# Two-layer streaming encoder on one core: product-key gates in spans of 3, 5, 8 and of 8, 8 blocks, and the scoring pools at the other end of SBUF

## The chip, the core and the metric

The kernel runs on one core of one Trainium2 chip. Its engines are TensorE (PE; its weight loads are listed apart as PEld), VectorE (DVE), ScalarE (ACT), GpSimd (POOL), which here only issues indirect transfers, and SyncE (SP), which issues the others. The metric is the device time of one execution in microseconds (us). [...]

## The reference, cut to what matters

Each of two layers is a mixer (attention, mLSTM, chunk MLP) and then a product-key expert layer (`peer`) over 16384 experts. Each token scores 2 x 128 sub-keys in 8 heads, takes the best 16 experts of each head, and adds a gated sum of their rows:

```
s = jnp.einsum('thcd,hckd->thck', q, keys)
v1, i1 = lax.top_k(s[:, :, 0], PEER_TOPK)
v2, i2 = lax.top_k(s[:, :, 1], PEER_TOPK)
...
e = i1[ci // 16] * 128 + i2[ci % 16];  g = softmax(vs)
act = gelu(einsum('thkd,td->thk', u_tab[e], xi))
y   = einsum('thk,thkd->td', g * act, v_tab[e])
```

There are 512 prompt tokens (four blocks of 128, b0 to b3) and 64 sample tokens (s). Everything is float32.

## The kernel before

**Two ways through the expert layer.** In each layer one pair of prompt blocks (b0 and b1 in layer 0, b2 and b3 in layer 1) meets all experts *densely*: the 16384 experts are 128 chunks of 128, and for each chunk TensorE makes H (eight products of a 128x128 piece of `U` with the tokens), ScalarE the gelu `A`, VectorE `A * W` with the gate block `W` (L1077), and TensorE adds `A`'s products with the chunk of `V` into `y` (L1084). Each chunk loads 512 KB of `U` and 512 KB of `V`. The other tokens *gather*: 64 pairs (s) or 128 pairs (a block) of rows from `peer_u` and from `peer_v`, 512 KB at a time, through four row buffers (`gath`). POOL issues a gather when a row buffer is free; VectorE multiplies the row (L964 for u, L976 for v) and so frees it. That is 640 gathers a layer.

**The gates.** A gate block `W` holds the gates of 8 chunks for 256 tokens. `gate_batch` builds, for 8 tokens, a one-hot of the second index (`o2`, 128x1024, L1002), one of the first index over the chunks of a *span* of blocks (`o1`, L1003) and its product with the gate (L1005); TensorE multiplies the two (L1009, 16 products), and ScalarE copies the result to each block of the span (L1011). 32 batches make a span, so `o2` and the 16 products are made once for each batch of each span, however many blocks it has. Before the change both layers have five spans (`QB`): of 1, 3, 4, 4, 4 and of 2, 2, 4, 4, 4 blocks. `first_gate` builds the first span ahead of the chunks; each further one is woven into the last `WIN` = 16 chunks of the span before it.

**Order.** A scheduler of the language fixes each engine's order at build time; every engine runs its list in that order. Gathers have low priority and fill the places that the scheduler's own clock leaves them. VectorE's list therefore holds the gathers' multiplies between the gates, the selection and the chunks' multiplies, and each waits for what stands ahead of it. Calls of `behind` add that a chunk's multiply stands after the last gate batch issued ahead of it.

**Layer 0**: mixer; `first_gate`; 8 chunks of the dense loop woven with `scores` of b2 and b3 (16 rounds of products, and `select_heads` on VectorE, L894 to L905); `finish_select`; the other 120 chunks. Gathers of s, b2 and b3 run beside it and on into layer 1's mixer. **Layer 1**: mixer; `scores` of b2 and b3 with 24 leads (H and gelu of the first chunks, 16 of them kept in `pre`); `first_gate`; 128 chunks. Gathers of s, b0 and b1 run beside it. Last comes `final` (a norm and a store) for each token block.

The tiles of `scores` and of the selection stand in the pool `select`, which is open through the whole program, and in `xg2`, `tmp2` and `wts2`.

Of the kernel before, what the change touches and what calls it, by code (L numbers as in the profile page):

```python
# [21 lines left out]
P = 128  # L22
DM = 1024
# [13 lines left out]
WT = 1056  # L37
TD = 256
NG = TD + NS
QB = [[1, 3, 4, 4, 4], [2, 2, 4, 4, 4]]  # L40
WIN = 16
LOW = 10 ** 7
PS_TAG = {"p": "mm", "a": "mm", "r": "mm", "o": "o", "tp": "tr", "ta": "tr", "tr": "tr"}
PS_BUFS = {"mm": 4, "tr": 3, "o": 1}
T_TAG = {"p": "t", "a": "t", "r": "tr"}
T_BUFS = {"t": 4, "tr": 2}
DENSE_T = 4
# [68 lines left out]

# Tokens go in groups: g1 = two prompt blocks and the sample, g2 = two prompt blocks. In each layer one pair of
# prompt blocks meets all experts densely (gates built from one-hot products); the other tokens gather their rows.
class Build:
    def __init__(self, ctx, tc, h, outs):  # L120
        self.tc, self.nc, self.h, self.o = tc, tc.nc, h, outs
        ec = ctx.enter_context
        self.cp = ec(tc.tile_pool(name="const", bufs=1))
        self.lp = ec(tc.tile_pool(name="layer", bufs=1))
        self.ca = ec(tc.tile_pool(name="carry", bufs=1))
        self.gp = ec(tc.tile_pool(name="gath", bufs=4))
        self.sm = ec(tc.tile_pool(name="small", bufs=2))
        self.dp = ec(tc.tile_pool(name="dram", bufs=1, space=DRAM))
        self.sp = ec(tc.tile_pool(name="select", bufs=1))

# [14 lines left out]
    def dense_pools(self, ec, l):  # L145
        tc = self.tc

        def pool(name, bufs, **k):
            return ec(tc.tile_pool(name=name, bufs=bufs, reuse_waits="tile", **k))
        self.dx = pool("xd", 1)  # L150
        self.up = pool("ustream", 2)
        self.vp = pool("vstream", 2)
        self.da = pool("act", 2)
        self.xg = pool("xg2", 1)
        self.t2 = pool("tmp2", DENSE_T)
        self.wp = pool("wts2", 3)
        self.whp = None
        self.wb = pool("gate", 5)
        self.d2 = pool("onehot", 2)
        self.py = pool("py", 1, space=PSUM)  # L160
        self.ph = pool("ph", 1, space=PSUM)
        self.pm = pool("pmm2", 1, space=PSUM)
        self.mixer = False

# [60 lines left out]

# [1 line left out]
    def setup(self):  # L227
# [92 lines left out]

# [278 lines left out]
    def mlstm(self, l, L, g):  # L599
# [65 lines left out]
        for sl, n in spans:  # L665
            w = sl.stop - sl.start
# [3 lines left out]
        for i, t in sorted(enumerate(g), key=lambda z: -1 if z[1].sample else z[0]):  # L670
            n, a, b = t.n, t.c0, t.c0 + t.n
# [21 lines left out]
            for hh in range(NH):  # L693
                c, r0 = hh // 2, (hh % 2) * HD
# [22 lines left out]
        for sl, n in spans:  # L717
            w = sl.stop - sl.start
# [12 lines left out]
        for sl, n in spans:  # L731
            w = sl.stop - sl.start
# [46 lines left out]

# [1 line left out]
    def scores(self, l, L, g):  # L781
# [231 lines left out]

    def gate_block(self, b):
        pool, tag = (self.wb, "W") if b % 6 else (self.ca, "W0")
        W = pool.tile([P, 8, TD], F32, tag=tag, name=tag)
        return W

    def first_gate(self, l):
        nb = QB[l][0]  # L1020
        self.W0 = [self.gate_block(i) for i in range(nb)]
        hots = None
        if nb == 1:
            hot = self.wb.tile([P, 4, P, 8], F16, tag="W", name="hot")
            o1s = hot[:, 3].rearrange("p i t -> p (i t)")
            hots = [(hot[:, i], o1s[:, 192 * i:192 * i + 192].rearrange("p (a i t) -> p a i t", a=3, i=8)) for i in range(3)]
        for t0 in range(0, TD, 8):
            self.gate_batch(self.W0, 0, t0, self.psum([8, 8 * nb]), hots and hots[t0 // 8 % 3])
            self.gated = self.mark
            yield  # L1030

    def peer_dense(self, l, group, xT):
        nc, h, lag = self.nc, self.h, LAG[l]
        ys = [self.py.tile([P, 2, 512], F32, tag=f"y{i}", name=f"y{i}") for i in range(len(group))]
        hh = self.ph.tile([P, 2, TD], F32, tag="H", name="H")
        pbs = self.ph.tile([P, 2, 8, 32], F32, tag="pb", name="pb")
        acts, pre, nl = [], [], 0
# [64 lines left out]
    def run(self):  # L1102
# [146 lines left out]
```

## Time and profile before

| what | value |
|---|---|
| three timed runs, median | 3788.93 us (3788.86 to 3792.08) |
| profiled execution, first to last instruction | 3795.5 us |
| PE / DVE / ACT / POOL busy | 3337.5 / 2703.0 / 713.3 / 1497.2 us |
| moved by the DMA engines | 1060.62 MB, mean 279 GB/s |

The profiled execution's own time is its span, 3795.5 us; it is 6.6 us (0.17%) above the median of the timed runs, and nothing more is listed around it. A busy share is an average over stages with different limits; the table of stages among the rows below is the view to start from. On POOL one instruction (x) is one gather.

### The profile page before, as it was taken

What the parts mean: (1) busy time and instruction counts of PE and PEld (TensorE: products, weight loads), DVE (VectorE), ACT (ScalarE), POOL (GpSimd) and SP (SyncE); (2) the same over time, 40 slices, a digit from 0 to 9 for tenths busy, and PEclk for the clock granted to TensorE, in tenths of its full rate; (3) what the DMA queues carried; (4) which work ended last, traced back from release to release, by engine and by line L of the source; (5) the groups of instructions that cost most, each with busy time, mean ns of one, the idle gap of its engine ahead of it and who ended that gap; (6) DMA issues with size and microseconds to landing.
All of it is one profiled execution on the core that took longest, in us unless ns stands there. A gap on an engine that the chain in (4) does not pass through costs nothing.

```text
span 3795.5 us, 48023 instructions
## 1 busy us (share of the span) xinstructions
PE 3337.5 (88%) x16456; PEld 2328.2 (61%) x16456; DVE 2703.0 (71%) x6490; ACT 713.3 (19%) x2594; POOL 1497.2 (39%) x1284
## 2 busy tenths in 40 slices
PE   8989889899999999979847787587758999999998
PEld 6767568667676676644524554266634766767764
DVE  4555877998667576555786997789887765766754
ACT  5444222111011011002211212121111111101100
POOL 0000004444444444445555245544565444444442
PEclk9999979899999999989868896698867999999999
DMA  5232227888999999999878698888888899999996
GB/s 178 97 107 70 88 79 259 309 308 301 368 329 326 362 318 348 362 330 328 269 254 303 227 340 249 294 292 305 274 282 276 307 352 337 321 352 335 324 368 247
DMA packets 299956, 1060.62 MB, mean 279 GB/s; under 512 B 36372, under 2 KB 39232, under 8 KB 299712
## 3 DMA queue, kind: packets, MB, share of 16 engines
q0 software_dynamic: 184320, 671.17, 50.3%
q1 hardware_dynamic: 115392, 386.38, 28.6%
q8 instruction: 131, 2.15, 0.2%
q14 instruction: 113, 0.93, 0.1%
HBM read 1048.09 MB, written 8.27 MB: 278 GB/s over the span
## 4 chain that ended last, share of the span: by engine, by line
PE 56%; DVE 16%; DMA 16%; issue 7%; POOL 4%; ACT 1%; SPq 0%; POOLq 0%; DVEq 0%; ACTq 0%
PE H L1044 19%; PE y L1084 19%; DMA row<-in_peer_v_dram,idx 8%; DMA row<-in_peer_u_dram,idx 5%; PE ps L381 5%; PE pb L1009 5%; DVE row L964 4%; POOL row L940 4%; PE ps L392 2%; DVE x_b L976 2%; DMA U<-in_uT_dram 1%; DMA V<-in_peer_v_dram 1%; PE ps L1009 1%; DVE x_s L976 1%; DVE i L895 1%
## 5 line engine op out<-in xcount | busy, mean ns | idle before, releaser
L940 POOL DMA_INDIRECT row<-in_peer_u_dram,idx x640 | 740.2, 1157 | 1439.6 <-DVE row L964 730.9
L940 POOL DMA_INDIRECT row<-in_peer_v_dram,idx x640 | 756.8, 1182 | 814.4 <-DVE x_b L976 452.4
L964 DVE SCALAR_TENSOR_TENSOR row<-row,xn 128x1024 f32<-128x1024 f32 x640 | 777.0, 1223 | 209.4 <-DMA row<-in_peer_u_dram,idx 206.4
L1084 PE MATMUL y<-V,A 128*128 128x512 f32 x1920 | 883.7, 603 | 15.9 <-DMA V<-in_peer_v_dram 12.1
L976 DVE SCALAR_TENSOR_TENSOR x_b<-row,hb,x_b 128x1024 f32<-128x1024 f32 x512 | 656.0, 1281 | 206.9 <-DMA row<-in_peer_v_dram,idx 203.1
L1084 PEld LDWEIGHTS y<-V,A 128*128 128x128 f32 x1920 | 361.8, 194 | 381.2 <-issue 357.9
L1044 PE MATMUL H<-xT,U 128*128 128x256 f32 x2048 | 482.6, 388 | 30.7 <-DMA U<-in_uT_dram 17.6
L1044 PE MATMUL H<-xTd,U 128*128 128x256 f32 x2048 | 478.9, 385 | 1.0 <-DMA U<-in_uT_dram 1.0
L1044 PEld LDWEIGHTS H<-xT,U 128*128 128x128 f32 x2048 | 391.3, 194 | 112.8 <-issue 43.4
L1044 PEld LDWEIGHTS H<-xTd,U 128*128 128x128 f32 x2048 | 388.2, 193 | 84.7 <-issue 38.7
L1009 PEld LDWEIGHTS <-o 128*128 128x128 f16 x4608 | 330.7, 161 | 158.7 <-DVE o L1005 76.8
L392 PE MATMUL ps<-xT,w 128*128 128x320 f32 (+1 forms) x1280 | 344.5, 425 | 38.3 <-DMA w<-in_wt_dram 18.8
L1002 DVE TENSOR_TENSOR o<-jj,sel 128x1024 f16<-128x1024 f16 x288 | 198.8, 691 | 201.0 <-PE pb L1009 169.7
L1009 PE MATMUL pb<-o,o 128*128 128x32 f16 (+2 forms) x4096 | 299.1, 235 | 39.9 <-DVE o L1005 31.9
L392 PEld LDWEIGHTS ps<-xT,w 128*128 128x128 f32 x1280 | 249.4, 199 | 109.3 <-ACT ssg L823 17.0
L1053 ACT ACTIVATE A<-H 128x256 f32<-128x256 f32 x240 | 92.1, 384 | 1012.4 <-PE H L1044 803.7
L1011 ACT ACTIVATE W<-pb 128x64 f32<-128x64 f32 x928 | 151.6, 289 | 668.6 <-PE pb L1009 611.1
L1077 DVE TENSOR_TENSOR A<-A,W 128x256 f32<-128x256 f32 x240 | 98.8, 425 | 139.0 <-ACT A L1053 130.7
L976 DVE SCALAR_TENSOR_TENSOR x_s<-row,hb,x_s 128x1024 f32<-128x1024 f32 x128 | 163.8, 1280 | 43.6 <-DMA row<-in_peer_v_dram,idx 43.0
L381 PE MATMUL ps<-w,xT 128*128 128x512 f32 (+3 forms) x320 | 128.5, 553 | 5.3 <-DMA w<-in_wn_dram 5.3
L336 DVE TENSOR_TENSOR wl<-w,wh 128x1024 fp32r<-128x1024 f32 (+1 forms) x56 | 64.4, 1150 | 76.5 <-PE ps L381 56.8
L381 PE MATMUL ps<-w,mix 128*128 128x512 f32 (+1 forms) x224 | 110.3, 646 | 5.6 <-DMA w<-in_wn_dram 4.0
(319 smaller groups left out, 3201.7 us busy)
## 6 DMA issues: line engine op xcount, KB each, us to landing
V<-in_peer_v_dram SPq DMA_DIRECT2D x256, 512.0 KB
U<-in_uT_dram SPq DMA_DIRECT2D x256, 512.0 KB
w<-in_wt_dram SPq DMA_DIRECT2D x96, 512.0 KB
w<-in_wn_dram SPq DMA_DIRECT2D x80, 512.0 KB
row<-in_peer_u_dram,idx POOLq DMA_INDIRECT x640
row<-in_peer_v_dram,idx POOLq DMA_INDIRECT x640
w<-in_keysT_dram SPq DMA_DIRECT2D x16, 256.0 KB
w<-in_wn_dram SPq DMA_DIRECT2D x8, 264.0 KB
```

The source lines that it names most:

```text
L381: self.nc.tensor.matmul(p[:t.n, :wd], x[kk][:, t.c0:t.c0 + t.n], ww[:, k * wd:(k + 1) * wd], start=(kk + part + j == 0), stop=(kk == KC - ...
L392: self.nc.tensor.matmul(ps, ww[:, k * P:(k + 1) * P], x[k][:, :n], start=(k + part + j == 0), stop=(k == KC - 1 and part == pair and j == ...
L940: self.nc.gpsimd.indirect_dma_start(out=row, out_offset=None, in_=self.h[tab], in_offset=bass.IndirectOffsetOnAxis(ap=t.idx[:, k:k + 1], a ...
L964: nc.vector.scalar_tensor_tensor(row, row, 1.0, xn, op0=ALU.mult, op1=ALU.mult, accum_out=hb[:, k:k + 1])
L976: op = nc.vector.scalar_tensor_tensor(x, row, t.hb[:, k:k + 1], x, op0=ALU.mult, op1=ALU.add)
L1002: nc.vector.tensor_tensor(o2, self.jj, self.sel[:, 1, None, t0:t0 + 8].to_broadcast([P, P, 8]), op=ALU.is_equal)
L1009: nc.tensor.matmul(pb[:, j, :nq], o2[:, :, j], o1[:, p, :, j], start=(p == 0), stop=(p == 1))
L1011: nc.scalar.activation(W[:, :, t0:t0 + 8].rearrange("p i t -> p t i"), pb[:, :, 8 * i:8 * i + 8], AF.Copy, scale=1.0 / GSCALE)
L1044: mm = nc.tensor.matmul(hp, U[:, k, :], xT[k], start=(k == 0), stop=(k == KC - 1))
L1053: nc.scalar.activation(a, hp, AF.Gelu)
L1077: gated = nc.vector.tensor_tensor(a, a, Ws[ci // 8][:, ci % 8, :], op=ALU.mult)
L1084: nc.tensor.matmul(ys[i][:, hf, :], a[:, i * P:(i + 1) * P], V[:, hf * 512:(hf + 1) * 512], start=(c == 0), stop=(c == NCH - 1))
```

## The change

Layer 0 now has three spans (3, 5, 8 blocks) and layer 1 two (8, 8); windows are 16 and 24 chunks in layer 0 and 24 in layer 1. `HOME` names a pool for each block: `0` the carried one, `a` the pool `gate` (5 buffers), `b` a new pool `gate2`. `gate2` is opened by `close_scores`, right after `finish_select`, where `select`, `xg2`, `tmp2` and `wts2` stood, and these now lie at the right end of SBUF. The one-hot `o1` of all batches but layer 0's first span is a tile of `gate2` too. A batch's PSUM tile now comes from the general tag, of three banks instead of two; the bank `pb` is gone. `first_gate` of layer 0 has four one-hot buffers instead of three.

```diff
-QB = [[1, 3, 4, 4, 4], [2, 2, 4, 4, 4]]
-WIN = 16
+QB = [[3, 5, 8], [8, 8]]
+WIN = [[16, 24], [24]]
+GATE_A, GATE_B = 5, [6, 5]
+HOME = ["0aaaaabbbbbb0aaa", "0aaabbbbbaa0aaab"]
...
+    def select_pool(self):
+        self.sel_es = ExitStack()
+        self.sp = self.sel_es.enter_context(self.tc.tile_pool(name="select", bufs=1, side="right", reuse_waits="tile"))
...
-        self.wb = pool("gate", 5)
+        self.wb = pool("gate", GATE_A)
...
+        ec = self.sel_es.enter_context
+        self.xg = pool("xg2", 1, side="right")
+        self.t2 = pool("tmp2", DENSE_T, side="right")
+        self.wp = pool("wts2", 3, side="right")
+
+    def close_scores(self, ec, l):
+        self.sel_es.close()
+        self.wb2 = ec(self.tc.tile_pool(name="gate2", bufs=GATE_B[l], side="right", reuse_waits="tile"))
...
-        ps = self.pm.tile([P] + list(shape), F32, tag=tag, name="ps", bufs=PS_BUFS[tag] if self.mixer else 2)
+        ps = self.pm.tile([P] + list(shape), F32, tag=tag, name="ps", bufs=PS_BUFS[tag] if self.mixer else 3)
...
-            o1 = self.d2.tile([P, 3, 32, 8], F16, tag="o1", name="o1")[:, :, :nq, :]
+            o1 = self.wb2.tile([P, 3, 64, 8], F16, tag="o1", name="o1", bufs=2)[:, :, :nq, :]
...
-        pbs = self.ph.tile([P, 2, 8, 32], F32, tag="pb", name="pb")
...
-            win = min(WIN, nq)
+            win = WIN[l][q] if more else 0
...
-                    self.gate_batch(nxt, c - ci + nq, 8 * done, pbs[:, done % 2])
+                        nxt = [self.gate_block(l, c // 8 - ci // 8 + nb + i) for i in range(QB[l][q + 1])]
+                    self.gate_batch(nxt, c - ci + nq, 8 * done, self.psum([8, 8 * len(nxt)]))
...
                     run(self.finish_select(l, g2))
+                    self.close_scores(es.enter_context, l)
```

**Place 1: VectorE, layer 0, from the end of the first gates to chunk 9.** Before, where `hot` and `o_...` are one-hots of the first and second span, `xn` the normed rows of s that gathers are multiplied by, `row` a gathered row, `A` a chunk's activations:

```order
L1002 TENSOR_TENSOR hot<-jj,sel 128x1024
L1005 TENSOR_TENSOR hot<-hot,sel 128x128
L956 SCALAR_TENSOR_TENSOR xn<-x_s,rs_y,row 64x1024
L1005 TENSOR_TENSOR o_5685<-o_5685,sel 128x2x192
...
L1077 TENSOR_TENSOR A<-A,W_4309 128x256 x3
L1005 TENSOR_TENSOR o_5709<-o_5709,sel 128x2x192
L964 SCALAR_TENSOR_TENSOR row,hb<-row,xn 128x1024 x8
...
L898 MAX_INDEX i_6261<-v_6260,s 128x8
L1002 TENSOR_TENSOR o_6936<-jj,sel 128x1024
L1003 TENSOR_TENSOR o_6937<-jj,sel 128x256
L1077 TENSOR_TENSOR A<-A,W 128x256 x2
```

The last row is chunks 9 and 10 of the dense loop. Counted over all rows up to there, 46 gate batches stand ahead of `xn`, and 58 gathers' multiplies ahead of chunk 9's. Now, in the same stretch (`x_s` is the sample's rows, `es`, `oh` and `idx` are of `finish_select` of b2 and b3):

```order
L966 SCALAR_TENSOR_TENSOR xn<-x_s,rs_y,row 64x1024
L1087 TENSOR_TENSOR A<-A,W_4311 128x256 x4
L974 SCALAR_TENSOR_TENSOR row,hb<-row,xn 128x1024 x6
...
L945 TENSOR_TENSOR es<-oh 128x128
L986 SCALAR_TENSOR_TENSOR x_s<-row,hb,x_s 128x1024
L896 SCALAR_TENSOR_TENSOR idx<-es 128x128
L986 SCALAR_TENSOR_TENSOR x_s<-row,hb,x_s 128x1024
L1013 TENSOR_TENSOR o_6064<-jj,sel 128x320
...
L1015 TENSOR_TENSOR o_6064<-o_6064,sel 128x2x320
L1015 TENSOR_TENSOR o_6091<-o_6091,sel 128x2x320
L1087 TENSOR_TENSOR A<-A,W 128x256
```

32 batches now stand ahead of `xn`. The last row is chunk 9: all selection of b2 and b3 and 105 gathers' multiplies stand ahead of it, since the first `o1` tiles of `gate2` take the place of the selection's.

**Place 2: VectorE, layer 1, start of the dense loop.** Before:

```order
L1003 TENSOR_TENSOR o_18530<-jj,sel 128x128
L1005 TENSOR_TENSOR o_18500<-o_18500,sel 128x2x128
L1077 TENSOR_TENSOR pre<-pre,W_17704 128x256
L976 SCALAR_TENSOR_TENSOR x_b_76<-row,hb,x_b_76 128x1024
L218 SCALAR_TENSOR_TENSOR rs_y<-rs_t,rs_y 128x1
L1005 TENSOR_TENSOR o_18530<-o_18530,sel 128x2x128
```

Now:

```order
L1087 TENSOR_TENSOR pre<-pre,W_16438 128x256 x8
L1087 TENSOR_TENSOR pre<-pre,W 128x256 x8
L1087 TENSOR_TENSOR A<-A,W 128x256 x10
...
L1015 TENSOR_TENSOR o_18161<-o_18161,sel 128x1024
L986 SCALAR_TENSOR_TENSOR x_b_73<-row,hb,x_b_73 128x1024 x30
L1087 TENSOR_TENSOR A<-A,W 128x256
```

The multiplies of 26 chunks stand in one piece; behind them come 35 gathers' multiplies, then one chunk at a time. 900 gathers' multiplies of all 1280 stood ahead of layer 1's first chunk, and 906 do now.

**Place 3: VectorE, end of its list.** Before (L1098 is the product that `final` ends with):

```order
L1077 TENSOR_TENSOR A<-A,W 128x256
L976 SCALAR_TENSOR_TENSOR x_b_78<-row,hb,x_b_78 128x1024 x9
L213 TENSOR_SCALAR rs_v<-ss 128x1
...
L1098 SCALAR_TENSOR_TENSOR y<-x_b_78,rs_y,fg 128x1024
L1091 TENSOR_TENSOR x_b_83<-y_16649,x_b_83 128x1024
L1091 TENSOR_TENSOR x_b_85<-y_16650,x_b_85 128x1024
```

Now:

```order
L1087 TENSOR_TENSOR A<-A,W 128x256
L986 SCALAR_TENSOR_TENSOR x_b_75<-row,hb,x_b_75 128x1024 x20
L1101 TENSOR_TENSOR x_b_80<-y_15377,x_b_80 128x1024
L986 SCALAR_TENSOR_TENSOR x_b_75<-row,hb,x_b_75 128x1024
L1101 TENSOR_TENSOR x_b_82<-y_15378,x_b_82 128x1024
L986 SCALAR_TENSOR_TENSOR x_b_75<-row,hb,x_b_75 128x1024 x26
...
L1108 SCALAR_TENSOR_TENSOR y<-x_b_75,rs_y,fg 128x1024
...
L1108 SCALAR_TENSOR_TENSOR y<-x_b_80,rs_y,fg 128x1024
```

Behind the last chunk's multiply stood nine gathers' multiplies, and 47 do now; all three last norms follow them. In layer 0, 420 stood ahead of the last chunk's multiply and 441 do now.

## Rows read from the trace of the kernel before

**Rows 1.** The page: granted clock in 40 slices; the chain that ended last, by engine.
```profile
PEclk9999979899999999989868896698867999999999
...
PE 56%; DVE 16%; DMA 16%; issue 7%; POOL 4%; ACT 1%; SPq 0%; POOLq 0%; DVEq 0%; ACTq 0%
```
**Rows 2.** Busy time by stage; the ends are the moments in rows 3.
```profile
core 0: us, PE busy (x) PEld busy (x) DVE busy (x) ACT busy (x) POOL busy (x), PEclk, DMA share, GB/s
513.00:587.00 74.00, 73.89 (x858) 68.86 (x858) 49.13 (x158) 25.73 (x103) 0.00 (x0) 0.73 0.13 41
587.00:728.00 141.00, 125.75 (x764) 102.89 (x763) 120.88 (x406) 29.74 (x127) 68.64 (x58) 0.91 0.85 304
728.00:1664.00 936.00, 928.07 (x4431) 644.84 (x4430) 654.06 (x1221) 118.37 (x532) 409.68 (x363) 1.00 0.93 337
1664.00:2156.00 492.00, 351.85 (x1270) 204.59 (x1269) 361.61 (x816) 97.35 (x332) 260.07 (x216) 0.82 0.84 288
2156.00:2797.00 641.00, 449.91 (x2131) 328.03 (x2130) 541.89 (x1619) 117.89 (x374) 310.54 (x263) 0.80 0.82 283
2797.00:3740.00 943.00, 914.55 (x4595) 624.01 (x4596) 653.09 (x1042) 114.65 (x556) 437.25 (x373) 0.96 0.91 329
```
**Rows 3.** Timeline of VectorE: first gather, chunks 9, 128, 129 and 256.
```profile
586.57 1.22 DVE L964 SCALAR_TENSOR_TENSOR row<-row,xn 128x1024 f32<-128x1024 f32 x1
728.70 0.75 DVE L1077 TENSOR_TENSOR A<-A,W 128x256 f32<-128x256 f32 x2
1664.37 0.43 DVE L1077 TENSOR_TENSOR A<-A,W 128x256 f32<-128x256 f32 x1 [2.77 <-ACT A L1053]
2797.55 0.42 DVE L1077 TENSOR_TENSOR pre<-pre,W 128x256 f32<-128x256 f32 x1
3739.72 0.43 DVE L1077 TENSOR_TENSOR A<-A,W 128x256 f32<-128x256 f32 x1 [1.18 <-ACT A L1053]
```
**Rows 4.** A stretch without gates in layer 0: all, then L1084 alone.
```profile
1480.00:1645.00 165.00, 165.00 (x577) 109.40 (x576) 90.17 (x118) 9.19 (x24) 72.52 (x66) 1.00 0.97 363
...
1480.00:1645.00 165.00, 86.03 (x193) 36.44 (x192) 1.00 0.97 363
```
**Rows 5.** A stretch with one window of gates: L1084 alone, then L1009 alone.
```profile
1224.00:1479.00 255.00, 116.80 (x258) 47.86 (x257) 1.00 0.93 338
...
1224.00:1479.00 255.00, 36.55 (x496) 36.33 (x496) 1.00 0.93 338
```
**Rows 6.** Timeline of TensorE: one batch of 32 and one of 8 columns.
```profile
3542.61 1.17 PE L1009 MATMUL pb<-o,o 128*128 128x32 f16 x16
...
520.22 1.10 PE L1009 MATMUL ps<-hot 128*128 128x8 f16 x16
```
**Rows 7.** Groups by line and shape: VectorE's part of a gate batch.
```profile
L1002 DVE TENSOR_TENSOR o<-jj,sel 128x1024 f16<-128x1024 f16 x288 | 198.8, 691 | 201.0 <-PE pb L1009 169.7 <-PE ps L1009 15.2 <-issue 10.7
L1005 DVE TENSOR_TENSOR o<-o,sel 128x512 f16<-128x512 f16 x192 | 80.7, 421 | 1.7
L1005 DVE TENSOR_TENSOR o<-o,sel 128x256 f16<-128x256 f16 x64 | 17.4, 285 | 0.0
L1003 DVE TENSOR_TENSOR o<-jj,sel 128x128 f16<-128x128 f16 x64 | 13.9, 219 | 0.0
```
**Rows 8.** Scoring rounds of layer 1, L392 alone; 256 rows are 16 rounds.
```profile
2480.00:2592.00 112.00, 62.91 (x256) 50.08 (x255) 0.94 0.84 296
```
**Rows 9.** Timelines of the end: last y products, last gathers, the norms of ScalarE.
```profile
3772.74 7.11 PE L1084 MATMUL y<-V,A 128*128 128x512 f32 x16 [0.28 <-DMA V<-in_peer_v_dram]
...
3740.07 1.28 DVE L976 SCALAR_TENSOR_TENSOR x_b<-row,hb,x_b 128x1024 f32<-128x1024 f32 x1
3754.33 3.93 DVE L976 SCALAR_TENSOR_TENSOR x_b<-row,hb,x_b 128x1024 f32<-128x1024 f32 x3 [3.73 <-DMA row<-in_peer_v_dram,idx]
...
3779.48 1.06 ACT L223 ACTIVATE y<-x_b 128x1024 f32<-128x1024 f32 x1 [19.98 <-DVE x_b L1091]
3787.22 1.06 ACT L223 ACTIVATE y<-x_b 128x1024 f32<-128x1024 f32 x1 [6.59 <-DMA out_dram<-y]
```

More of the change, by code (lines that the diff above doesn't have):

```diff
@@ L128, in __init__ @@
         self.dp = ec(tc.tile_pool(name="dram", bufs=1, space=DRAM))
-        self.sp = ec(tc.tile_pool(name="select", bufs=1))
+    def select_pool(self):
+        self.sel_es = ExitStack()
+        self.sp = self.sel_es.enter_context(self.tc.tile_pool(name="select", bufs=1, side="right", reuse_waits="tile"))
     def mixer_pools(self, ec, l):
@@ L153, in dense_pools @@
         self.da = pool("act", 2)
[L154 to L157, printed above, removed]
-        self.wb = pool("gate", 5)
+        self.wb = pool("gate", GATE_A)
         self.d2 = pool("onehot", 2)
@@ L162, in dense_pools @@
         self.pm = pool("pmm2", 1, space=PSUM)
-        self.mixer = False
+        self.whp, self.mixer = None, False
+        ec = self.sel_es.enter_context
[5 more added lines that the diff above has]
+        self.wb2 = ec(self.tc.tile_pool(name="gate2", bufs=GATE_B[l], side="right", reuse_waits="tile"))
     def psum(self, shape, st="p"):
         tag = PS_TAG[st] if self.mixer else "mm"
-        ps = self.pm.tile([P] + list(shape), F32, tag=tag, name="ps", bufs=PS_BUFS[tag] if self.mixer else 2)
+        ps = self.pm.tile([P] + list(shape), F32, tag=tag, name="ps", bufs=PS_BUFS[tag] if self.mixer else 3)
         return ps
@@ L323, in wload @@
         n = src.shape[1]
-        w = self.wp.tile([P, DM if self.whp else WT], F32, tag="w", name="w")
+        w = self.wp.tile([P, WT if self.mixer and not self.whp else DM], F32, tag="w", name="w")
         self.nc.sync.dma_start(w[:, :n], src)
@@ L1012, in gate_batch, with gate_block @@
                                  scale=1.0 / GSCALE)
-    def gate_block(self, b):
-        pool, tag = (self.wb, "W") if b % 6 else (self.ca, "W0")
+    def gate_block(self, l, b):
+        home = HOME[l][b]
+        pool, tag = (self.ca, "W0") if home == "0" else (self.wb if home == "a" else self.wb2, "W")
         W = pool.tile([P, 8, TD], F32, tag=tag, name=tag)
@@ L1020, in first_gate @@
         nb = QB[l][0]
-        self.W0 = [self.gate_block(i) for i in range(nb)]
         hots = None
-        if nb == 1:
+        if l == 0:
             hot = self.wb.tile([P, 4, P, 8], F16, tag="W", name="hot")
-            o1s = hot[:, 3].rearrange("p i t -> p (i t)")
-            hots = [(hot[:, i], o1s[:, 192 * i:192 * i + 192].rearrange("p (a i t) -> p a i t", a=3, i=8)) for i in range(3)]
+            hot1 = self.wb.tile([P, 4, 3, 8 * nb, 8], F16, tag="W", name="hot1")
+            hots = [(hot[:, i], hot1[:, i]) for i in range(4)]
+        self.W0 = [self.gate_block(l, i) for i in range(nb)]
         for t0 in range(0, TD, 8):
-            self.gate_batch(self.W0, 0, t0, self.psum([8, 8 * nb]), hots and hots[t0 // 8 % 3])
+            self.gate_batch(self.W0, 0, t0, self.psum([8, 8 * nb]), hots and hots[t0 // 8 % 4])
             self.gated = self.mark
@@ L1069, in peer_dense @@
                     if not nxt:
-                        nxt = [self.gate_block(c // 8 - ci // 8 + nb + i) for i in range(QB[l][q + 1])]
-                    self.gate_batch(nxt, c - ci + nq, 8 * done, pbs[:, done % 2])
+                        nxt = [self.gate_block(l, c // 8 - ci // 8 + nb + i) for i in range(QB[l][q + 1])]
+                    self.gate_batch(nxt, c - ci + nq, 8 * done, self.psum([8, 8 * len(nxt)]))
                     done += 1
@@ L1116, in run @@
             self.sel = self.ca.tile([P, 4, TD], F16, tag="sel", name="sel")
+            self.select_pool()
             with ExitStack() as es:
@@ L1146, in run @@
                     run(self.finish_select(l, g2))
+                    self.close_scores(es.enter_context, l)
                     run(self.first_gate(l))
```

## The prediction

> **What bounds the kernel now.** I read the chain first, then a table of stages, then single rows. The chain is 56% TensorE, with VectorE and transfers at 16% each [rows 1]: no one engine carries it. The stages say why [rows 2]. From 728 to 1664 us (dense loop of layer 0) TensorE is busy in 928 of 936 us and the DMA engines at 0.93; in the dense loop of layer 1 it is 915 of 943. In between, for 1133 us, TensorE is busy 70% and its clock is 0.8. What never pauses is the gather stream. POOL's counts give its pace in each stage: 141/58 = 2.43 us a gather, 936/363 = 2.58, 492/216 = 2.28, 641/263 = 2.44, 943/373 = 2.53. It does not go below 2.28 even where TensorE leaves the DMA engines room, because four row buffers limit it, and VectorE's list ties it to everything else: a chunk's multiply cannot pass the gathers listed ahead of it. So I work the time out along VectorE's list, from one moment to the next [rows 3]: at each step either the listed gathers are late or TensorE is.
>
> **Prices.** Without gates TensorE is busy for the whole stretch, and 193/8 = 24.1 chunks take 165 us: 6.84 us a chunk, 3.42 for the H half or the y half, with a gather every 165/66 = 2.50 us [rows 4]. With a window of gates 258/8 = 32.25 chunks and 496/16 = 31 batches take 255 us [rows 5]: (255 - 32.25 x 6.84)/31 = 1.11 us a batch. A batch of 8 columns spans 1.10 us and one of 32 spans 1.17 [rows 6], so the columns cost nearly nothing. No row has 40 or 64 columns: from below 1.11 us, from above in proportion to the columns, 2.22 us for 64. The 8-to-32 rows are nearest; I take 1.11. [...] On VectorE a batch's `o2` costs 0.69 us, and its `o1` parts go from 0.219 us for 128 elements to 0.421 for 512 [rows 7], 0.53 ns an element. ScalarE copies every block as before: nothing.
>
> Saved on TensorE: 64 batches in layer 0's loop and 96 in layer 1's, 178 us. Little of it is the gain, since the gathers remain.
>
> **The change, moment by moment** (spans of the profiled execution, 3795.5 us; the median is 3788.9, so the difference found is taken from the median).
>
> *First gather's multiply, before 586.6 [rows 3].* 46 batches stood ahead of `xn` in some 74 us [rows 2], 1.6 each; 32 do now. 14 x 1.6 = -22; the 32 have 384 more elements of `o1` each, 32 x 0.2 = +6. So 15 us earlier: 572.
>
> *Chunk 9, before 728.7 [rows 3].* This is the step that loses. All selection of b2 and b3 and 105 gathers now stand ahead of it, for the room of `gate2` comes free only then; before, chunks and gates ran between them. TensorE has little to do meanwhile. 104 paces of 2.4 (between 2.28 and 2.58; 2.43 is the row where VectorE had this same selection) = 250: 822, 93 us later. Bounds 809 and 840.
>
> *Chunk 128 of layer 0, before 1664.4.* Behind chunk 9 TensorE has 120 y halves, 115 H halves (13 chunks' H stand ahead in its list) and 64 batches: 235 x 3.42 + 64 x 1.11 = 804 + 71 = 875. The 336 gathers in between need 336 x 2.50 = 840, so TensorE sets it. y ends at 1697. The last multiply comes some three chunks earlier, as `LAG` is 2: 1677, 13 us later than before. With 2.22 for 64 columns and 1.39 for 40, 44 more. 441 gathers are now done by then, not 420.
>
> *Chunk 129, before 2797.6.* Layer 1's mixer, scoring and first gate: 1133 us for 900 - 420 = 480 gathers, 2.36 each. 465 remain: -35 if the gathers set it all, 0 if the mixer's own chain does. The first gate has 8 blocks instead of 2: 128 becomes 512 elements and 256 becomes 1024, (0.42 + 0.69) - (0.22 + 0.285) = 0.61 us x 32 = +20 on VectorE [rows 7], which is 85% busy there [rows 2]. I take -15, with bounds -35 and +20: 1677 + 1118 = 2795. The copies of 8 blocks, six more for each batch, lie beside VectorE's work.
>
> *Chunk 256, before 3739.7, 942 us later.* TensorE: 128 y and 101 H halves (27 stand ahead) and 32 batches = 783 + 36 = 819 to the end of y, and the multiply comes 40 us before that as in the rows (3739.7, and y to 3779.9 [rows 3, 9]), so 779. Gathers listed: 1233 - 906 = 327 at 2.53 = 827. So the gathers set it: 3622. The bytes, (327 + 128 + 101) x 0.524 MB = 291 MB, make 352 GB/s, under the 363 of [rows 4]. Bounds 2.50 and 2.58: 818 and 844.
>
> *The tail.* 47 gathers instead of nine. The nine took from 3740.1 to 3758.3 [rows 9], 2.0 each: 94, so 3716. [...]
>
> *The norms.* b1's, b2's and b3's all follow the last gather now: 7.7 us from one to the next and 8.3 from the last to the end [rows 9], 24: **3740**. Before, the end was 16 us behind y.
>
> The difference is 55 us: 3788.9 - 55 = **3734**.
>
> What costs nothing: the third PSUM bank for a batch (it can only take a wait away), SBUF addresses at the start of layer 1's mixer (the weights now lie where gate blocks end early; before, some lay under the last gate blocks; a gain of one load at most, a few us), and the fourth one-hot buffer. The cover is TensorE, or the gathers; if it is gone, each costs one wait for a buffer, under 10 us. SP's list keeps its loads in the order of the chunks.
>
> **Rivals.**
>
> *A. Chunk 9 is held much longer, and the time is slower than before.* With the dense loop standing still, TensorE has gaps between scoring rounds, and its clock could go to the lower of its levels; selection then waits for scores. At a clock of 0.94 the 16 rounds took 112 us in layer 1 [rows 8]; 16 halves of chunks come to 55, and the last quarter of selection with its finish to some 60. At full clock 572 + 167 + 60 = 799, which the gathers hide. At a clock of 0.6, 572 + 278 + 60 = 910, 88 us past my moment, all of which goes to y's end: 3822. It decides from chunk 9 at 877, a clock of 0.68. For it: slices of 95 us at 0.6 do occur [rows 1]. Against: stages in which TensorE is 70% busy show 0.80 and 0.82 [rows 2], and 0.8 gives 841. 0.15.
>
> *B. The batches take time by their columns.* 44 us more in layer 0; in layer 1 36 on TensorE, still under the gathers: 3778. Rows 6 speak against it. 0.06.
>
> *C. The gathers pace better once VectorE and TensorE have less to do.* 2.28 up to chunk 9 (-13), all 15 gathers saved up to chunk 129 (-20), 2.50 in layer 1 (-9): 3692. For it: 160 fewer `o2` of 0.69 us, 110 us less on VectorE [rows 7]. Against: 2.28 already has an idle quarter of VectorE. 0.16.
>
> *D. The gain is lost again.* Chunk 9 by a pace of 2.58 (+18), chunk 129 after +10 instead of -15 because the mixer's own chain counts (+25), 2.55 in layer 1 (+7): +50, 3784. This is also where the change does nothing: what TensorE saves, the gather stream gives back as a tail. 0.09.
>
> **How the numbers follow.** My sum has 0.54. The forecast is its time, 3734. B's end and C's stand within 60 us; A reaches over 3800. The range from 3690 to 3800 leaves out most of A and the far side of C, some 0.2. Within 0.2% (7.6 us, about what this measurement can tell) lies most of D and a little of A; slower is A. Faster: 0.54 + 0.16 + 0.05 = 0.75; same 0.10; slower 0.15.
>
> **What would show it.** In the profile after: the first gather's multiply near 572; chunk 9's near 822, with TensorE's busy share well under 0.8 and its clock around 0.8 from 590 to there; without gates still 6.84 us a chunk; 1.1 us a batch of 64 columns; chunk 128 near 1677 and chunk 129 near 2795, hardly moved; chunk 256 near 3622, more than 100 us earlier; then some 47 gathers alone, about 94 us, and three norms in a row. I am wrong if chunk 9 comes after 860, if layer 1's loop stays over 880 us, or if the tail's pace is far from 2.0.

## The result, and the profile after

| | before | after | ratio (95%) |
|---|---|---|---|
| first comparison, median | 3788.89 us | 3823.64 us (3814.97 to 3846.74) | 1.0106 (1.0068 to 1.0143) |
| second comparison, later (chip 14) | 3793.28 us | 3818.00 us (3814.93 to 3840.70) | 1.0078 (1.0051 to 1.0105) |
| profiled execution, span | 3795.5 us | 3845.0 us | |

The kernel got about 1% slower; the forecast was 3734 us, 1.45% faster. The span of the profiled execution of after is itself 21 us above the median.

Timeline of VectorE after: first gather, chunks 9, 128, 129 and 256; it answers to [rows 3]. Forecast were 572, 822, 1677, 2795 and 3622.

```profile
573.17 1.22 DVE L974 SCALAR_TENSOR_TENSOR row<-row,xn 128x1024 f32<-128x1024 f32 x1
...
820.22 0.42 DVE L1087 TENSOR_TENSOR A<-A,W 128x256 f32<-128x256 f32 x1
...
1730.25 0.47 DVE L1087 TENSOR_TENSOR A<-A,W 128x256 f32<-128x256 f32 x1 [1.09 <-ACT A L1063]
...
2867.80 1.43 DVE L1087 TENSOR_TENSOR pre<-pre,W 128x256 f32<-128x256 f32 x4
...
3721.79 0.43 DVE L1087 TENSOR_TENSOR A<-A,W 128x256 f32<-128x256 f32 x1 [1.30 <-ACT A L1063]
```

The first two moments are met within 2 us. The third is 53 us late, and from there the delay grows by 20 and by 27 us. Against the moments of before, chunk 9 comes 92 us later; the loop of layer 0 is 26 us shorter, the stage behind it 4 longer, the loop of layer 1 88 shorter, and what follows it 67 longer: 49 us in all (3845.0 - 3795.5). Busy time by stage after, as [rows 2], cut at these moments:

```profile
core 0: us, PE busy (x) PEld busy (x) DVE busy (x) ACT busy (x) POOL busy (x), PEclk, DMA share, GB/s
...
573.00:820.00 247.00, 136.87 (x603) 107.71 (x603) 210.83 (x665) 26.71 (x93) 122.55 (x105) 0.77 0.83 286
820.00:1730.00 910.00, 907.98 (x3801) 629.53 (x3801) 553.67 (x858) 108.84 (x542) 396.02 (x336) 0.99 0.91 330
1730.00:2868.00 1138.00, 835.14 (x3385) 562.69 (x3384) 907.19 (x2404) 234.21 (x894) 572.19 (x466) 0.81 0.82 276
2868.00:3722.00 854.00, 831.81 (x3076) 548.62 (x3075) 507.34 (x704) 78.04 (x366) 390.83 (x328) 0.99 0.92 336
3722.00:3845.00 123.00, 37.29 (x71) 15.00 (x69) 71.92 (x86) 3.45 (x6) 51.02 (x44) 0.66 0.70 239
```

In the stage from 820 to 1730 TensorE hardly pauses (908 of 910 us) and its clock is 0.99, with the 336 gathers that the forecast counted: TensorE does the work that was counted, and takes longer for it. The last stage (47 gathers and three norms) is 123 us, forecast 118.

A stretch after with one window of 64 columns: all, then L1094 alone, then L1019 alone; it answers to [rows 5].

```profile
1013.00:1293.00 280.00, 280.00 (x1235) 202.10 (x1234) 174.82 (x309) 46.35 (x270) 114.79 (x98) 0.99 0.88 310
...
1013.00:1293.00 280.00, 116.32 (x259) 48.97 (x260) 0.99 0.88 310
...
1013.00:1293.00 280.00, 61.48 (x464) 56.46 (x462) 0.99 0.88 310
```

259/8 = 32.4 chunks and 464/16 = 29 batches, by the prediction's method: (280 - 32.4 x 6.84)/29 = 2.01 us a batch, not 1.11. The timeline of TensorE shows it without a sum: runs of products of 40 and of 64 columns.

```profile
865.20 1.02 PE L1019 MATMUL ps<-o,o 128*128 128x40 f16 x11
...
2783.99 4.01 PE L1019 MATMUL ps<-o,o 128*128 128x64 f16 x32 [6.46 <-DVE o L1015]
...
2815.59 2.08 PE L1019 MATMUL ps<-o,o 128*128 128x64 f16 x16 [0.20 <-DVE o L1015]
```

A batch of 16 products spans 2.08 us where [rows 6] had 1.17 for 32 columns. By the start times of single products, the median from one start to the next (products of the same width, one behind the other) is 60 ns for 24 columns (504 products), 77 for 40 (494) and 120 for 64 (1451); before, it was 60 for 8 to 24 and 62 for 32. That fits a floor of 60 ns and, above it, 1.9 ns a column (77/40 and 120/64).

### The profile page after: what moved, and what is told of

The parts are those of the page before. It is cut to its first block, busy times and chain, and to the rows that moved or that the text cites. A ratio compares the mean times of both kernels' runs of the same rounds, so it can differ in the third digit from the quotient of the medians.

```text
span 3845.0 us, 42498 instructions
## 1 busy us (share of the span) xinstructions
PE 3266.1 (85%) x13896; PEld 2260.0 (59%) x13896; DVE 2588.9 (67%) x6010; ACT 683.9 (18%) x2590; POOL 1536.7 (40%) x1284
## 4 chain that ended last, share of the span: by engine, by line
PE 60%; DMA 16%; DVE 13%; issue 6%; POOL 3%; ACT 1%; SPq 0%; POOLq 0%; DVEq 0%; ACTq 0%
PE H L1054 22%; PE y L1094 21%; DMA row<-in_peer_v_dram,idx 7%; PE ps L1019 5%; PE ps L391 4%; DMA row<-in_peer_u_dram,idx 4%; PE ps L402 3%; POOL row L950 3%; DVE row L974 3%; DMA V<-in_peer_v_dram 2%; DMA U<-in_uT_dram 1%; DVE x_b L986 1%; PE ps L567 1%; PE ps L569 1%; DMA w<-in_wt_dram 1%
## 5 line engine op out<-in xcount | busy, mean ns | idle before, releaser
L950 POOL DMA_INDIRECT row<-in_peer_v_dram,idx x640 | 791.4, 1237 | 793.6 <-DVE x_b L986 459.2
L1094 PE MATMUL y<-V,A 128*128 128x512 f32 x1920 | 877.6, 601 | 20.5 <-DMA V<-in_peer_v_dram 18.1
L1094 PEld LDWEIGHTS y<-V,A 128*128 128x128 f32 x1920 | 367.3, 193 | 394.0 <-issue 380.4
L1019 PE MATMUL ps<-o,o 128*128 128x64 f16 (+1 forms) x2048 | 244.7, 288 | 145.7 <-DVE o L1015 140.1
L1019 PEld LDWEIGHTS <-o 128*128 128x128 f16 x2048 | 226.7, 145 | 191.5 <-issue 125.3
L1021 ACT ACTIVATE W<-ps 128x64 f32<-128x64 f32 x1024 | 149.1, 311 | 474.4 <-PE ps L1019 382.5
L1012 DVE TENSOR_TENSOR o<-jj,sel 128x1024 f16<-128x1024 f16 x128 | 88.2, 690 | 143.4 <-PE ps L1019 134.9
```

Source lines behind the costliest of these rows:

```text
L950: self.nc.gpsimd.indirect_dma_start(out=row, out_offset=None, in_=self.h[tab], in_offset=bass.IndirectOffsetOnAxis(ap=t.idx[:, k:k + 1], a ...
L1012: nc.vector.tensor_tensor(o2, self.jj, self.sel[:, 1, None, t0:t0 + 8].to_broadcast([P, P, 8]), op=ALU.is_equal)
L1019: nc.tensor.matmul(pb[:, j, :nq], o2[:, :, j], o1[:, p, :, j], start=(p == 0), stop=(p == 1))
L1021: nc.scalar.activation(W[:, :, t0:t0 + 8].rearrange("p i t -> p t i"), pb[:, :, 8 * i:8 * i + 8], AF.Copy, scale=1.0 / GSCALE)
L1094: nc.tensor.matmul(ys[i][:, hf, :], a[:, i * P:(i + 1) * P], V[:, hf * 512:(hf + 1) * 512], start=(c == 0), stop=(c == NCH - 1))
```

## Experiments

In `o1`, laid out as [3, columns, 8 tokens], the columns of one product (one token) lie 8 values of 2 bytes, 16 bytes, apart. Two theories say why a wide product is dear. **S:** the step of 16 bytes makes each column cost 1.9 ns, hidden under the floor up to 32 columns. **C:** 64 columns cost that in any layout. For the rest of the miss, **G** says that the gathers give back what TensorE wins or loses, and **M** that layer 1's mixer has its own pace, so that a lead or a delay stays. Chips differ (the median of before is 3806.15 us on chip 5, 3793.28 on chip 14 and 3797.10 on chip 4), so ratios are to the kernel before on the same chip.

**Columns side by side.**

```diff
-o1 = ...tile([P, 3, 64, 8], F16)[:, :, :nq, :]
+o1 = ...tile([P, 3, 8, 64], F16)[:, :, :, :nq]
...
-    matmul(pb[:, j, :nq], o2[:, :, j], o1[:, p, :, j], ...)
+    matmul(pb[:, j, :nq], o2[:, :, j], o1[:, p, j, :], ...)
```

VectorE's two `o1` instructions now write in the new order, too: the compare reads `jj` at every eighth value and repeats each value of `sel` along the columns; the multiply repeats each value of `sel`.

> The changed kernel, with o1 laid out so that the columns of one product lie side by side (2 bytes apart) and not 16 bytes apart; nothing else differs. In the changed kernel's trace a gate product takes 60 ns from start to start with 24 columns, 77 with 40 and 120 with 64. Theory S (the 16-byte step of the moving operand makes a column cost 1.9 ns, hidden up to 32 columns under a floor of 60 ns): every product takes about 60 ns, the dense loop of layer 0 from chunk 9 to chunk 128 takes 870 us instead of 910, that of layer 1 is 15 to 30 us shorter, the whole about 3765 us (3740 to 3790). Theory C (64 columns cost that much in whatever layout): 64 columns stay at 120 ns, 3816 to 3832. VectorE's o1 parts may get slower by the other order, which would show in the first gate of layer 1 (at most some 25 us).

Ratio 1.004 (0.9999 to 1.008). Here are one batch on TensorE, and from the groups by line and shape VectorE's two `o1` instructions:

```profile
2793.07 1.16 PE L1020 MATMUL ps<-o,o 128*128 128x64 f16 x16 [1.17 <-ACT W L1022]
...
L1016 DVE TENSOR_TENSOR o<-o,sel 128x1024 f16<-128x1024 f16 x96 | 116.6, 1220 | 0.5
L1013 DVE TENSOR_TENSOR o<-jj,sel 128x512 f16<-128x512 f16 x96 | 102.4, 1067 | 0.0
```

S holds and C falls: 64 columns take 1.16 us a batch, 61 ns from start to start, like 8 or 32. The loops took 882 and 832 us (910 and 854 in the changed kernel). The total, some 3804 us where before takes 3789, misses S's 3740 to 3790 all the same. VectorE now takes 1.07 and 1.22 us where the changed kernel takes 0.42 and 0.69, and the stage of layer 1's mixer and first gate became 1165 us.

**The same layout in the kernel before**, whose products have at most 32 columns (the same edit, with 32 for 64).

> The kernel before, with the same other layout of o1. Its products have 8 to 32 columns and take 60 ns. Theories S and C both expect no change of the products (60 ns) and of the time (within 8 us of 3789): it is the control that shows what the layout costs on VectorE by itself. If it gets faster, the step of 16 bytes had cost something below 32 columns too.

Products stayed at 60 ns, and the ratio was 1.008 (1.0042 to 1.0118): outside what was expected. VectorE's 512-element part took 0.688 us here against 0.421 in [rows 7], its 128-element part 0.373 against 0.219:

```profile
L1006 DVE TENSOR_TENSOR o<-o,sel 128x512 f16<-128x512 f16 x192 | 132.1, 688 | 1.2
L1003 DVE TENSOR_TENSOR o<-jj,sel 128x128 f16<-128x128 f16 x64 | 23.8, 373 | 0.0
```

So the layout by itself costs, and all its use comes from wide products.

**Columns 4 and 8 bytes apart**, with runs of 2 and of 4 tokens left for VectorE.

```diff
+o1 = ...tile([P, 3, 2, 64, 4], F16)[:, :, :, :nq]        (8 bytes; 4, 64, 2 for 4 bytes)
...
+for p in range(2):
+    tensor_tensor(o1[:, p], o1[:, 2], sel[2 + p] in runs of 4, op=ALU.mult)
...
+    matmul(pb[:, j, :nq], o2[:, :, j], o1[:, p, j // 4, :, j % 4], ...)
```

> The changed kernel, with the 8 tokens of a batch split in o1 so that the columns of a product lie 4 bytes apart, and pairs of tokens side by side, so that VectorE's operands keep runs of 2. With the columns 2 bytes apart a 64-column product took 60 ns, but VectorE's o1 parts went from 0.42 and 0.69 us to 1.07 and 1.22. Theory S in its sharper form (the price of a column goes with the step, 1.9 ns at 16 bytes, 0.5 at 4): 60 ns again, layer 0 from chunk 9 to 128 in 875 to 885 us (910 in the changed kernel). If VectorE keeps its quick rate (0.42 us for 512, two halves of 0.42 for 1024), the first gate of layer 1 is not longer than in the changed kernel and the whole is 25 to 60 us under it; if not, it is as with 2 bytes, some 30 longer there.

> As the one with 4 bytes, with the columns 8 bytes apart and runs of 4 tokens. A look for the price of a product alone. If the price goes in proportion to the step, 64 columns at 8 bytes take 64 x 0.94 = 60 ns, just the floor; if any step above 2 bytes costs the same, 120 ns.

With 4 bytes the ratio was 0.9915 (0.9886 to 0.9943), faster than before; the single execution with 8 bytes took 3734.96 us where the kernel before had a median of 3793.28. One batch on TensorE and VectorE's 512-element parts, first with 4 bytes, then the compare with 8:

```profile
2745.40 1.32 PE L1020 MATMUL ps<-o,o 128*128 128x64 f16 x16 [0.60 <-DVE o L1017]
...
L1017 DVE TENSOR_TENSOR o<-o,sel 128x512 f16<-128x512 f16 x192 | 73.6, 427 | 0.7
L1014 DVE TENSOR_TENSOR o<-jj,sel 128x512 f16<-128x512 f16 x96 | 58.4, 610 | 0.0
```

```profile
2732.22 1.34 PE L1020 MATMUL ps<-o,o 128*128 128x64 f16 x16 [0.81 <-DVE o L1017]
...
L1014 DVE TENSOR_TENSOR o<-jj,sel 128x512 f16<-128x512 f16 x96 | 39.9, 417 | 0.0
```

From start to start these are 60 and 63 ns. With 4 bytes the loop of layer 0 took 871 us, a little under what was expected, and the whole was 60 us under the changed kernel on the same chip, the far end of the 25 to 60, although VectorE's compare stayed at 0.61 us. At 8 bytes VectorE is back at 0.42 us: both engines have their quick rate (63 ns a product, 0.42 us a compare). A price of 0.94 ns a column at 8 bytes would be just the floor at 64 columns (60 ns), so the 63 ns bound the price there at about 1 ns a column and don't show that it is nothing.

**Columns 32 bytes apart, in the kernel before** (`[P, 3, 32, 16]`, one buffer).

> The kernel before with its columns 32 bytes apart in place of 16 (every second group of 16 bytes unused; one o1 buffer instead of two, for room). A look for the price of a product alone; the time is longer for the single buffer too. If the price is columns times step (16 bytes: 1.9 ns a column), 32 columns take 120 ns, 24 take 90 and 16 take 60. If every step of 16 bytes or more costs 1.9 ns, all stay at 60.

```profile
1237.33 1.17 PE L1009 MATMUL pb<-o,o 128*128 128x32 f16 x16
```

32 columns stay at 64 ns from start to start, so my sharper form, a price in proportion to the step, is wrong above 16 bytes: a column costs at most 64/32 = 2.0 ns at 32 bytes, not 3.8. No run has more than 32 columns at that step, so what a column costs there above the floor is not shown. (With its single buffer the whole took 3949.9 us; that time is not used.)

**The 8-byte kernel, timed.**

> The kernel with columns 8 bytes apart once more, timed. Its one look went as the forecast for the changed kernel had it (chunk 128 at 1686 us, 129 at 2800, 256 at 3622, the end 3733). If the column price was the whole miss, the median is 0.985 of the kernel before (0.981 to 0.989) and the moments repeat within 15 us; if that look was a lucky execution, 0.991 like the 4-byte kernel.

Median 3756.78 us, ratio 0.9895 (0.9869 to 0.9921). That is between the two expectations. The first execution was quicker than all six here, but its moments repeat within 14 us and its end within 19. The kernel is faster than before; from the one with 4 bytes (0.9915) the intervals do not tell it apart. Its stages, then the stretch with the window of 64 columns (L1095, then L1020):

```profile
812.00:1683.00 871.00, 869.01 (x3801) 593.12 (x3801) 559.55 (x918) 107.67 (x543) 379.64 (x336) 1.00 0.94 344
1683.00:2814.00 1131.00, 807.33 (x3375) 536.95 (x3373) 912.73 (x2445) 231.86 (x893) 560.48 (x470) 0.81 0.83 280
2814.00:3633.00 819.00, 800.65 (x3082) 521.56 (x3083) 510.81 (x736) 77.40 (x366) 393.50 (x330) 1.00 0.95 351
3633.00:3752.00 119.00, 41.35 (x72) 16.48 (x70) 67.01 (x82) 3.48 (x7) 49.27 (x40) 0.65 0.68 231
...
1004.00:1248.00 244.00, 112.56 (x250) 47.47 (x251) 1.00 0.94 340
...
1004.00:1248.00 244.00, 33.72 (x445) 33.34 (x443) 1.00 0.94 340
```

(244 - 250/8 x 6.84)/(445/16) = 1.09 us a batch: the forecast's price. The two dense loops take 871 and 819 us where the changed kernel takes 910 and 854.

**The changed kernel again.**

> The changed kernel as it is, beside the others on the same chip. Its first profiled execution was 21 us above the median of its runs. Theory R (that execution's layer 1 mixer and first gate, 1138 us instead of the forecast's 1118, were long by the execution and not by the kernel): the interval between chunk 128 and chunk 129 comes out near 1120 this time, with chunk 9 to 128 again 910 and chunk 129 to 256 again 854. Rival (the first gate with 512 and 1024 elements on VectorE costs 20 us, the bound of the forecast): 1138 again.

```profile
820.00:1732.00 912.00, 907.04 (x3802) 628.21 (x3802) 553.55 (x859) 108.96 (x542) 393.52 (x337) 0.99 0.91 330
1732.00:2838.00 1106.00, 808.44 (x3381) 546.95 (x3381) 905.22 (x2403) 233.73 (x893) 567.08 (x465) 0.83 0.83 284
2838.00:3696.00 858.00, 835.63 (x3077) 550.73 (x3076) 506.90 (x704) 77.66 (x365) 396.36 (x327) 0.98 0.91 334
```

The loops repeat within 4 us (912 and 858). The stage between them is 1106 us here and was 1138: theory R holds as far as two executions can show it. The stage differs by 32 us between them, and the forecast's 1118 lies in between.

**Layer 0's spans as before, layer 1 in 8, 8** (16 bytes; layer 0's windows, batch banks and the place of `o1` are as before too, so chunk 9 is not held).

```diff
-QB = [[3, 5, 8], [8, 8]]
+QB = [[1, 3, 4, 4, 4], [8, 8]]
-HOME = ["0aaaaabbbbbb0aaa", ...
+HOME = ["0aaaaa0aaaaa0aaa", ...
...
```

> The changed kernel with layer 0's spans, windows, homes and batch banks as before (1, 3, 4, 4, 4), layer 1 as changed (8, 8). Layer 0 then ends as before, y near 1686 us instead of 1748, with about 17 fewer gathers done by chunk 128. Theory G (between the dense loops the gather stream sets the time, 2.4 us each): the 62 us are given back but for 20, about 3800. Theory M (layer 1's mixer has its own pace): layer 0's loss was all of the loss, about 3765. If layer 1's part of the change is the whole loss: 3824.

Ratio 1.001 (0.9973 to 1.0046), 3793 us where before is 3789: nearer to G's 3800 than to M's 3765, which is outside the interval; so is 3824. Between chunks 128 and 129 it takes 1149 us with 483 gathers:

```profile
1682.00:2831.00 1149.00, 821.52 (x3391) 553.24 (x3390) 925.82 (x2437) 237.06 (x896) 590.73 (x483) 0.81 0.84 282
2831.00:3673.00 842.00, 825.73 (x3077) 548.13 (x3075) 502.80 (x702) 77.93 (x365) 387.34 (x325) 0.99 0.93 340
```

**Chunk 9 not held** (16 bytes).

```diff
-QB = [[3, 5, 8], [8, 8]]
+QB = [[3, 3, 5, 5], [8, 8]]
-WIN = [[16, 24], [24]]
+WIN = [[16, 24, 24], [24]]
...
+o1 = (self.wb2 if self.cols > 40 else self.d2).tile([P, 3, self.cols, 8], ...)
```

> The changed kernel with layer 0 in spans of 3, 3, 5, 5 blocks and o1 beside o2, so that no batch of the second span waits for the selection's room: chunk 9 stands behind 29 gathers and chunk 13 behind 75, not 105 and 118. Layer 1 as changed. TensorE then reaches chunk 128 near 1660 us instead of 1730, but with 402 gathers done, not 441. Theory M (layer 1's mixer sets its own time): the 70 us stay, about 3755. Theory G (the gathers set it, 39 more of them at 2.4 us, 94 us): nothing is won, 3825 to 3850.

Ratio 1.003 (0.999 to 1.0069), some 3800 us (3785 to 3815) where before is 3789: M's 3755 us is excluded, and so are G's 3825 to 3850. Neither theory holds by itself. Chunk 9 came at 643 us and chunk 128 at 1655, as expected, and the stage behind it took 48 to 80 us more than in the changed kernel, with 38 gathers more:

```profile
643.00:1655.00 1012.00, 987.03 (x4638) 697.34 (x4638) 695.94 (x1415) 134.11 (x599) 438.55 (x374) 0.99 0.91 324
1655.00:2841.00 1186.00, 815.67 (x3382) 552.43 (x3381) 950.42 (x2476) 232.81 (x892) 615.82 (x504) 0.80 0.84 282
```

**Both repairs, with 4 bytes.** The edits of the last one and of the 4-byte one together.

> Both repairs: layer 0 in spans of 3, 3, 5, 5 with o1 beside o2 (chunk 9 behind 29 gathers), layer 1 in 8, 8, and columns 4 bytes apart in both. Against the run without the hold and 16 bytes (1.003 of the kernel before) layer 0's 64 batches of 40 columns save 0.27 us each, 17 us, layer 1's loop about 20: 0.994 of the kernel before, 3765 on a chip where that takes 3789. If the gathers give all that back as a longer tail (theory G), 1.003 again.

Ratio 0.9906 (0.9878 to 0.9934), a little better than the expected 0.994, and 1.003 is excluded; a median of 3759.30 us beside 3758.41 for the 4-byte kernel that holds chunk 9, on one chip. The stage between the layers' loops, first here, then in that one:

```profile
1636.00:2816.00 1180.00, 801.61 (x3376) 535.74 (x3374) 957.18 (x2508) 231.77 (x893) 593.37 (x503) 0.79 0.83 283
```

```profile
1689.00:2815.00 1126.00, 793.61 (x3376) 528.61 (x3374) 918.40 (x2443) 231.87 (x894) 557.90 (x469) 0.82 0.82 281
```

53 us of lead at chunk 128 are used up by 34 gathers that are still to be done, and chunk 129 comes at the same time in both. This kernel also has 32 batches more, so the two runs don't price the hold by itself.

**The second window late** (8 bytes; `WIN = [[8, 24], [24]]` is the whole edit).

> Columns 8 bytes apart and one number changed: the second span's window is its last 8 chunks, not 16, so that chunks 9 to 16 wait for no batch; chunk 9 stands behind 29 gathers, not 103, and chunk 17 behind 115. Theory G (what TensorE does not do while it is held, the gathers do; total time is theirs): within 10 us of the kernel with 8 bytes, although chunk 128 may come up to 40 us earlier with fewer gathers done. Theory M (the hold is lost time): 25 to 45 us faster than it.

Ratio 0.9921 (0.9902 to 0.9940) beside 0.9895 without the edit, 13 us by the medians; G allowed 10, and M's gain did not come. The edit moves the hold more than it takes it away: chunk 9 came at 649 us, but chunk 17 at 858 behind 115 gathers, and chunk 128 at 1701, 18 us later than in the 8-byte kernel.

**Layer 1's spans as before** (8 bytes, layer 0 in 3, 5, 8).

```diff
-QB = [[3, 5, 8], [8, 8]]
+QB = [[3, 5, 8], [2, 2, 4, 4, 4]]
...
```

> Columns 8 bytes apart, layer 0 as changed (3, 5, 8), layer 1 in spans of 2, 2, 4, 4, 4 as before. If layer 1's long spans carry the gain (96 fewer batches in a loop that TensorE sets), its loop takes 900 to 940 us instead of 822, and the whole 3775 to 3795. If the gathers set the loop anyway, within 15 us of the kernel with 8, 8.

Ratio 0.9965 (0.9950 to 0.9979), 3785.41 us. Its loop in layer 1 and what follows it:

```profile
2801.00:3708.00 907.00, 900.00 (x4611) 620.13 (x4611) 639.54 (x1145) 116.07 (x558) 422.97 (x353) 0.99 0.93 332
3708.00:3783.60 75.60, 34.61 (x71) 13.90 (x69) 43.56 (x64) 3.45 (x6) 25.21 (x22) 0.78 0.65 231
```

907 us instead of 819, 900 of them TensorE's: the long spans' gain is TensorE's time in this loop. Of the 88 us of the loop some 29 are left in the medians (3785.41 against 3756.78). In the profiled executions the short spans win back 43 us behind the last chunk (76 us against 119), where 25 gathers are left and not 43, and 24 us in the stage ahead of the loop (1107 against 1131), whose first gate has 2 blocks and not 8.

## Why the prediction was wrong

**The step that failed** is the price of a batch, "the columns cost nearly nothing ... The 8-to-32 rows are nearest; I take 1.11". All rows that I had lay under a floor of 60 ns a product, and I carried the flat part on to 40 and 64 columns. A batch of 64 took 2.01 us, near the other end of my bounds (2.22), and one of 40 took 16 x 77 ns = 1.23 us in products alone. A second step failed with it, the overlap in layer 1, "So the gathers set it": what the batches cost there was not hidden under the gathers (chunk 256 below). None of the three signs by which I would be wrong came: chunk 9 was at 820, the loop of layer 1 took 854, and the tail's pace was 2.1 us. What told was the price of a batch of 64 columns.

*First gather, chunk 9.* Right: 573 for 572 and 820 for 822. TensorE's busy share was 0.55 and its granted clock 0.77 of the full one while chunk 9 was held; of 200 windows of 1.2 us in this stretch 88 show 0.50, 106 show 1.00 and six something in between. VectorE was busy for 211 of the 247 us, and all that it waited for were gathered rows, which came at 2.35 us each; it waited for no scores, so rival A did not happen (waits between these moments: us in total, times, longest):

```profile
DVE row L974 <- DMA row<-in_peer_u_dram,idx: 30.7, 25, 3.4
DVE x_s L986 <- DMA row<-in_peer_v_dram,idx: 4.1, 6, 1.3
```

*Chunk 128.* 53 us late. With the columns 8 bytes apart and the same 336 gathers, the loop is 871 us instead of 910: the column price is 39 of the 55 us by which it missed its 855. Of the other 16, six are the half chunk: 32 chunks without gates took 220.4 us (chunks 65 to 97), 3.44 a half and not 3.42, for 235 halves. The rest is in the trace of the 8-byte kernel: its last multiply comes 14 us ahead of the end of y (1683.0 and 1697.1), not 20, and TensorE waits for four, most of them for a chunk of `V`.

*Chunk 129.* 20 us off in the profiled execution and 12 the other way in the second one: right within the scatter of that stage. The profiled executions with a first gate of 8 blocks (but for the side-by-side one, whose VectorE was slower) show how it goes with the gathers left: in six of them 463 to 470 take 1106 to 1138 us; 483 take 1149, and 503 and 504 take 1180 and 1186. By the means, 1123 us for 467 gathers and 1183 for 503.5, a gather more costs about 60/36.8 = 1.6 us there, between M's nothing and G's 2.4.

*Chunk 256.* I had the gathers set this loop with 827 us, and rival B hid 36 us more of TensorE under them. The loop took 854 and 858 us, and 819 with 8 bytes: the 35 us were not hidden. TensorE is busy for 832 of 854 us, and its longest waits are for chunks of `V` (us in total, times, longest):

```profile
PE y L1094 <- DMA V<-in_peer_v_dram: 18.9, 11, 4.0
```

The right price alone does not repair the sum: with 2.01 us a batch my working gives TensorE 783 + 64 - 40 = 807 us, still under 827. It held TensorE's part too low (between the two moments lie 954/8 y and 1616/16 H halves, 220 in all: 757 + 64 = 821 us) and left out its waits. With 8 bytes TensorE is still busy for 801 of the 819 us, and where short spans in layer 1 give it more to do, it is busy for 900 and the loop takes 907. So it is TensorE that sets this loop, and that 819 lies near my 827, which I had from the gathers, is luck. Rival B's mechanism was right in both layers, with 39 us for its 44 in the first; its 44 us in all were too low by these 35. I gave it 0.06.

*The tail and the norms.* Right: 123 us for 118, 99 of them for the 47 gathers. That is 2.1 us each, near the 2.0 of the sum.

**With the one cause taken away, the forecast's sum comes back.** In the first execution of the 8-byte kernel chunk 128 came at 1686 us, 129 at 2800, 256 at 3622 and the end at 3733, against 1677, 2795, 3622 and 3740; the match of the third to the microsecond is luck, as said above. Over six executions it is 0.9895, which is 3749 us where before is 3789, 15 more than forecast: its profiled execution spans 12 us more than the sum of 3740, 13 of it in the stage between the loops.

**The step.** The runs show a price of 1.9 ns a column at a step of 16 bytes, at most 2.0 at 32 (64 ns for 32 columns), and 64 columns at the floor with 8, 4 and 2 (63, 60 and 61 ns). Why 16 bytes is the dear one they don't show: a price in proportion to the step up to 16 bytes and flat from there would give the same times as one that begins only at 16. The prediction had not weighed the step.

**VectorE in the side-by-side layout.** In the multiply one operand then repeats each value along the innermost direction, and 1024 elements took 1.22 us instead of 0.69. In the compare the other operand is also read at every eighth value, and 512 elements took 1.07 us instead of 0.42; no run parts these two. With innermost runs of 4 in both operands the compare was at 0.42 again (0.61 with runs of 2; a multiply of 512 with runs of 2 in one operand alone was at 0.43).

**Settled and open.** Shown: the price of wide products comes from the columns' step (64 columns: 120 ns at 16 bytes, 60 to 63 below); with 8 bytes the 1.0078 to 1.0106 become 0.9895; a lead at the end of layer 0's loop is mostly given back to the gathers. Not shown: why a step of 16 bytes is the dear one, and what the hold of chunk 9 costs by itself. The kernels without it either had more batches or moved it to a later chunk.

## What to carry to other kernels

- A flat row may be a floor that hides a second price. Before carrying a price to a larger size, look at the operand's layout for what could rise under the floor (here 32 columns x 1.9 ns = 60 ns, just the floor), and price both ends in the sum, not just in the range.
- Batching to save instructions pays less once the wider instruction leaves the floor: here 2.01 us for 64 columns, where two batches of 32 took 2.22. Bring the moving operand's elements closer together first (64 columns: 63 ns at 8 bytes, 120 at 16); keep runs of a few elements for the engine that writes them (a compare of 512: 0.42 us with runs of 4, 0.61 with runs of 2).
- Where a stream of transfers runs beside the bound, count how much of it is left at each moment: 53 us of lead with 34 gathers fewer done was no lead.

## What the runs showed of the hardware that was not expected

- TensorE, f16, 128 rows: a product with its own weight load takes 60 to 62 ns from start to start up to 32 columns of a moving operand whose columns lie 16 bytes apart, 77 ns at 40 and 120 at 64 (in the changed kernel the medians at 24, 40 and 64 columns are the same at a granted clock of 0.50 and of 1.00); at 2, 4 or 8 bytes it takes 60 to 63 ns at 64 columns; at 32 bytes, 64 ns at 32 columns, the widest tried. The weights themselves were read at a step of 16 bytes in all of these.
- VectorE, f16, two operands: 512 elements take 0.42 us with innermost runs of 4 or 8. With runs of 2 in one operand it is 0.43, with runs of 2 in both 0.61. With one operand repeated along the innermost direction 512 elements take 0.69 us and 1024 take 1.22; with the other read at every eighth value besides, 512 take 1.07.
